# Order of the second modulation step and the planner's first transfer in a decoder block on one core

## The chip, the cores and the metric

The kernel runs on one core of a Trainium2 chip. The metric is the device time of one execution in microseconds (us), as the median of several runs; lower is better. A core has TensorE (PE, matmuls), VectorE (DVE), ScalarE (ACT), GpSimd (POOL) and SyncE (SP), which here issues every transfer from HBM. The engines run side by side, each through its own list of instructions, and wait for each other by semaphores.

## The reference, cut to what matters

One decoder block, 512 tokens of 1024 channels, float32. Around the change only this of it matters:

```
mod = silu(c) @ W_ada + b_ada                    # 6 x 1024 values
shift1, scale1, gate1, shift2, scale2, gate2 = split(mod, 6)
h = rms_norm(x, g_pre_mix) * (1 + scale1) + shift1
z = h @ w_in                                     # 1024 -> 4800 columns
...
```

Behind it come a GLU with a causal convolution of 31 taps and a LayerNorm, a latent attention of 8 heads, a gated merge, and an MLP of 4096 hidden channels; both sub-layers add to x. `h` can't be formed before `shift1` and `scale1` are there, and these need 2 of the 6 megabyte blocks of each 128 channels of `W_ada`.

## The kernel before, in words

**Layout.** Activations are held transposed, a tile being 128 channels by 512 tokens; `h` is 8 such tiles, k = 0 to 7. Float32 products are made of three fp32r products: every operand is split into a high part (an ACT copy that rounds) and a low part (a DVE subtraction), and `mm3` adds high x high, high x low and low x high.

**The first stage.** `x` is loaded (4 tiles), normed and transposed on PE into `xnT`. Then, for each k, three things follow each other:

- The modulation of step k: the shift and scale columns of its 128 channels, from one megabyte of `W_ada` (`ada_load`, 4 transfers of 256 KB). For k = 0 and 1 PE makes them, with 8 float32 matmuls of 256 columns against the column `cT` of silu(c); a matmul of this kind shows as two records in the trace. ACT copies the row out, and `to_columns` turns it into columns by two small matmuls with ones. For k = 2 to 7 DVE makes the sums with 8 operations over 128x256, and only the two ones matmuls are on PE.
- `h` of step k, in `first_products(k)`: ACT writes the high part from `xnT` with scale and shift; DVE (k = 0, 1) or ACT (k from 2) writes the exact value, and DVE subtracts for the low part.
- The first products with `h` of step k: a 128x896 piece of `w_in` (`g1_load`, two transfers of 256 and 192 KB) is split by ACT and DVE, and 21 matmuls of 512 columns add to 7 banks of PSUM over all k.

All `ro`, ones and column reads use one PSUM bank, `bg`, so modulation k+1 can write into it only after DVE has read the columns of k.

**What sets the order.** Nothing is emitted in program order. `Planner.record` notes every operation with a cost and its dependences; `Planner.plan` then plays the engines through in an event loop, and `Planner.issue` (line 410, the line of nearly every row) emits the instructions in the order so found. An engine that is free takes, of its operations that are ready, the one with the smallest key. For PE the key is the rank, which is the position in the program minus `plan.boost`; for all others it is the due time `dead` minus `plan.hurry`. Due times are followed back from the sums of PE costs in program order. Each transfer takes its turn on one modelled stream, `dma_free`, which says from when it is free. The arenas for buffers are laid out anew in up to 14 passes from the lives that the last plan gave, and the shortest plan is kept. The planner's costs set the order alone: on the chip each engine runs its list and waits where its operands are late.

**Lines.** `dma_free = 0.0` is line 341, in `Planner.plan`. In `emit`: `ada_load` 544, `g1_load` 558, `to_columns` 657, `first_products` 669; the loads of k = 0 and 1 lines 689 to 696, the loop with their modulation 698 to 708, the two calls of `first_products` 711 and 712, and the loop for k = 2 to 7 lines 714 to 736. Because of the boost of 1000 in line 689, all PE operations of both modulations rank ahead of the products of k = 0.

Of the kernel before, what the change touches and what calls it, by code (L numbers as in the profile page):

```python
# [53 lines left out]
HX, HA, HG, HC = 1.2e5, 1e5, 3e3, 1.1e5  # L54
# [115 lines left out]
class Planner:  # L170
# [17 lines left out]
    class Engine:  # L188
        def __init__(self, plan, name):
            self.plan, self.name = plan, name  # L190
# [134 lines left out]
    def plan(self):  # L325
        ops = self.ops
        pe_t = 0.0
        big = sum(o.cost for o in ops if o.eng == "pe") + TAIL
        for o in ops:
            o.dead = big  # L330
            if o.eng == "pe":
                pe_t += o.cost
                o.dead = pe_t
        for o in reversed(ops):
            lat = o.post + (2.0 * o.dma if o.dma else 0.0)
            for s in o.succ:
                q = ops[s]
                o.dead = min(o.dead, q.dead - q.cost - lat)
        heaps = {e: [] for e in self.NAMES}
        free = {e: 0.0 for e in self.NAMES}  # L340
        dma_free = 0.0
        landed = [0.0] * DEPTH
        future = []

        def key(o):
            return (o.rank, o.i) if o.eng == "pe" else (o.dead - o.hurry, o.i)

        for o in ops:
            o.ndep, o.ready = len(o.deps), 0.0
            if not o.ndep:  # L350
                heapq.heappush(future, (0.0, o.i))
        order = []
        now = 0.0
        while len(order) < len(ops):
            while future and future[0][0] <= now:
                o = ops[heapq.heappop(future)[1]]
                heapq.heappush(heaps[o.eng], (key(o), o.i))
            for e in self.NAMES:
                if free[e] <= now and heaps[e]:
                    o = ops[heapq.heappop(heaps[e])[1]]  # L360
                    o.t0 = now
                    free[e] = now + o.cost
                    if o.dma:
                        st = max(now + 1100.0, dma_free)
                        dma_free = st + o.dma
                        o.t1 = dma_free + 1100.0
                        landed.append(o.t1)
                        free[e] = max(free[e], landed[-DEPTH])
                    else:
                        o.t1 = free[e] + o.post  # L370
                    order.append(o)
                    for s in o.succ:
                        q = ops[s]
                        q.ndep -= 1
                        q.ready = max(q.ready, o.t1 if (q.eng != o.eng or o.dma) else free[e] if e == "pe" else max(free[e], o.t1 - 30))
                        if not q.ndep:
                            heapq.heappush(future, (q.ready, q.i))
            nxt = [free[e] for e in self.NAMES if free[e] > now and heaps[e]]
            if future:
                nxt.append(future[0][0])  # L380
            if not nxt:
                break
            now = max(now, min(nxt)) if min(nxt) > now else now
        assert len(order) == len(ops)
        self.length = max(o.t1 for o in ops)
        return order
# [28 lines left out]
def tile_hybrid_block(  # L415
# [48 lines left out]
    def emit(past, replay):  # L464
# [3 lines left out]
        plan = Planner(nc, dict(f_arena=fa, r_arena=ra, psum=pb))  # L468
        pe, act, dve, pool, sp = (plan.engine(e) for e in Planner.NAMES)

        def rf(b, pat=None, **kw):
            a = RTF[:, b[0]:b[0] + b[1]]
            return a.rearrange(pat, **kw) if pat else a
# [84 lines left out]
        def g1_load(k):  # L558
            b = fa.alloc((NA + NB) * P)
            sp.dma_start(out=fa.v(b)[:, :NA * P], in_=w_in[k * P:(k + 1) * P, 0:NA * P])  # L560
            sp.dma_start(out=fa.v(b)[:, NA * P:], in_=w_in[k * P:(k + 1) * P, D:D + NB * P])
            return b
# [84 lines left out]
        def hs(k, a=0, n=T):  # L647
            return ra.v(hT[k][0])[:, a:a + n], ra.v(hT[k][1])[:, a:a + n]
# [8 lines left out]
        def to_columns(src, lp, ks):  # L657

            for s in range(2):
                for i, k in enumerate(ks):  # L660
                    pe.matmul(pb.v(bg)[:, s * KD + k:s * KD + k + 1], lhsT=src[:, s, i * P:(i + 1) * P], rhs=ones[0:lp, 0:1],
                              start=True, stop=True)
            ksl = slice(ks[0], ks[-1] + 1)
            dve.tensor_tensor(mod[:, 0, ksl], pb.v(bg)[:, ksl], col("bada", ks[0], len(ks)), ALU.add)
            for k in ks:
                dve.scalar_tensor_tensor(mod[:, 1, k:k + 1], pb.v(bg)[:, KD + k:KD + k + 1], b1p[:, k:k + 1], col("gpm", k),
                                         op0=ALU.add, op1=ALU.mult)

        def first_products(k, wb):
            v = fa.alloc(T)  # L670
            act.activation(ra.v(hT[k][0]), xv[:, k], AF.Identity, scale=mod[:, 1, k:k + 1], bias=mod[:, 0, k:k + 1])
            if k < VDVE:
                dve.tensor_scalar(fa.v(v), xv[:, k], mod[:, 1, k:k + 1], mod[:, 0, k:k + 1], ALU.mult, ALU.add)
            else:
                act.activation(fa.v(v), xv[:, k], AF.Identity, scale=mod[:, 1, k:k + 1], bias=mod[:, 0, k:k + 1])
            dve.tensor_tensor(ra.v(hT[k][1]), fa.v(v), rf(hT[k][0]), ALU.subtract)
            fa.free(v)
            w = W(fa.v(wb, "p (s n) -> p s n", s=1), 1, (NA + NB) * P)
            fa.free(wb)

            for wi, hi in ((0, 0), (0, 1), (1, 0)):
                for i in range(NA + NB):
                    o = i // 2 if i % 2 == 0 else NA + i // 2
                    pe.matmul(pb.v(g1b[i]), lhsT=w(0, o * P, P)[wi], rhs=hs(k)[hi], start=k == 0 and wi + hi == 0,
                              stop=k == KD - 1 and wi == 1)
            w.free()
# [6 lines left out]
        wbs = []  # L693
# [2 lines left out]
            wbs.append(g1_load(k))  # L696
        plan.hurry = HG
        for k in range(2):
            av = ad0[k][1]
            ro = pb.v(bg)[0:1, 256:512].rearrange("p (s n) -> p s n", s=2)  # L700
            for j in range(KD):
                pe.matmul(ro, lhsT=cT[:, j:j + 1], rhs=av[:, :, j], start=j == 0, stop=j == KD - 1)
            fa.free(ad0[k][0])
            acc = fa.alloc(2 * P)
            accv = fa.v(acc, "p (s n) -> p s n", s=2)[0:1]
            act.copy(accv, ro)
            to_columns(accv, 1, (k,))
            fa.free(acc)
        plan.boost = 0
        plan.hurry = 0.0  # L710
        for k in range(2):
            first_products(k, wbs[k])

        for ks in KGRP:
            plan.hurry = HA - 1e4 * ks[0]
# [4 lines left out]
            wbs = [g1_load(k) for k in ks]  # L720
# [690 lines left out]
        for tp in range(2):  # L1411
# [34 lines left out]
            for k2 in range(KD // 2):  # L1446
                b = pb.alloc()
                for q in range(2):
                    for t in range(2):
                        k = 2 * k2 + q  # L1450
                        pe.transpose(pb.v(b)[:, (2 * q + t) * P:(2 * q + t + 1) * P], fa.v(xn[t])[:, k * P:(k + 1) * P], ident)
                for q in range(2):
                    k = 2 * k2 + q
# [280 lines left out]
        return plan  # L1734

    plan = emit({}, {})
    plan.plan()
    best = plan
    for _ in range(PASSES):
        try:  # L1740
            plan = emit(plan.lives(), {})
        except MemoryError:
            break
        plan.plan()
        if plan.length < best.length:
            best = plan
    if plan is not best:
        plan = emit({}, {n: a.places for n, a in best.spaces.items()})
# [31 lines left out]
```

## Time and profile before

| | |
|---|---|
| median of 3 runs | 816.17 us (815.13 to 816.69) |
| the profiled execution, its own time | 815.82 us |
| its span, first to last instruction | 814.0 us |
| granted TensorE clock, mean | 0.998 of 2.4 GHz |
| busy: PE, PE weight loads | 796.5 us (98%), 681.1 us (84%) |
| busy: DVE, ACT, POOL | 732.2 us (90%), 441.6 us (54%), 22.0 us (3%) |
| moved by the transfers | 117.31 MB |

The span is what the trace shows of the execution; 1.8 us of its own time lie around it. Matmuls are pipelined and their ends are modelled: a PE that shows busy is not always at its full rate, so the pitch (time between starts, from counts and starts) says more than the busy share. "x30" behind a row is the number of instructions merged in it, the first column its start and the second its length; what stands in brackets is the idle time of the engine before it, and what ended that.

### The profile page before, as it was taken

How to read it: one execution, taken by the hardware profiler on the slowest of the kernel's cores; microseconds unless marked ns; L12 is line 12 of the kernel's file. 1: busy time of each engine (PE TensorE's matmuls, PEld its weight loads, DVE VectorE, ACT ScalarE, POOL GpSimd, SP SyncE). 2: the span in 40 equal slices, each digit the busy share in tenths (PEclk: the TensorE clock that was granted, in tenths of full speed). 3: DMA queues.
4: the chain of work that ended last, by engine and by line, in shares of the span. 5: the costliest groups of instructions: out<-in, count | busy, mean ns of one | idle time of the engine just before them, and what ended most of it. 6: DMA issues, size and time to landing. Idle time of an engine off the chain costs nothing.

```text
span 814.0 us, 11293 instructions
## 1 busy us (share of the span) xinstructions
PE 796.5 (98%) x4222; PEld 681.1 (84%) x4222; DVE 732.2 (90%) x1049; ACT 441.6 (54%) x735; POOL 22.0 (3%) x77
## 2 busy tenths in 40 slices
PE   6999999999999999999999999999999999999996
PEld 3778988889897888878888889988998889888885
DVE  3898999999999999998899589899889989996696
ACT  5455453365885247237434387676665547554543
POOL 2001010000000000000000010000000000000001
PEclk9999999999999999999999999999999999999999
DMA  9989433112253250451799253026403580590302
GB/s 296 314 257 320 148 122 104 52 53 65 91 182 80 77 151 31 155 170 63 268 316 369 77 202 112 2 78 199 137 2 98 186 292 18 163 301 2 104 1 103
DMA packets 91337, 117.31 MB, mean 144 GB/s; under 512 B 7473, under 2 KB 66194, under 8 KB 91282
## 3 DMA queue, kind: packets, MB, share of 16 engines
q1 hardware_dynamic: 91282, 116.59, 44.9%
q8 instruction: 33, 0.54, 0.3%
q14 instruction: 22, 0.18, 0.1%
HBM read 108.18 MB, written 8.39 MB: 143 GB/s over the span
## 4 chain that ended last, share of the span: by engine, by line
PE 84%; DVE 8%; ACT 3%; DMA 2%; issue 1%; POOL 1%; SPq 0%; DVEq 0%
PE psum L410 84%; DVE f_arena L410 5%; DVE r_arena L410 3%; ACT f_arena L410 2%; ACT r_arena L410 1%; DMA c<-in_c_dram 1%; DMA f_arena<-in_w_in_dram 1%; POOL stats L410 1%; ACT stats L410 0%; SPq L410 0%; DMA rows<-in_kv_norm_g_dram 0%; DVE mod L410 0%; DVEq L1775 0%; DVEq L410 0%
## 5 line engine op out<-in xcount | busy, mean ns | idle before, releaser
L410 PE MATMUL psum<-r_arena 128*128 128x512 f32 (+3 forms) x3880 | 756.4, 355 | 0.9 <-ACT r_arena L410 0.6
L410 PEld LDWEIGHTS psum<-r_arena 128*128 128x128 f32 x3880 | 640.1, 189 | 100.7 <-ACT r_arena L410 2.6
L410 ACT CAST r_arena<-f_arena 128x1024 fp32r<-128x1024 f32 (+4 forms) x240 | 224.9, 964 | 169.1 <-PE psum L410 115.3
L410 DVE TENSOR_TENSOR r_arena<-f_arena,r_arena 128x1024 fp32r<-128x1024 f32 (+4 forms) x250 | 265.9, 1089 | 31.2 <-PE psum L410 21.4
L410 DVE SCALAR_TENSOR_TENSOR f_arena<-f_arena,cw 128x512 f32<-128x512 f32 x240 | 165.8, 738 | 0.0
L410 DVE TENSOR_TENSOR f_arena<-f_arena 128x1024 f32<-128x1024 f32 (+3 forms) x99 | 102.3, 1047 | 3.0 <-ACT r_arena L410 1.6
L410 ACT ACTIVATE f_arena<-f_arena 128x512 f32<-128x512 f32 (+4 forms) x112 | 66.1, 606 | 29.0 <-DVE f_arena L410 27.9
L410 ACT ACTIVATE f_arena<-psum 128x512 f32<-128x512 f32 x52 | 30.6, 594 | 71.9 <-PE psum L410 71.3
L410 DVE SCALAR_TENSOR_TENSOR f_arena<-f_arena,cT 128x256 f32<-128x256 f32 (+1 forms) x70 | 56.0, 801 | 7.4 <-DMA f_arena<-in_w_ada_dram 6.4
L410 DVE TENSOR_TENSOR f_arena<-psum,f_arena 128x512 f32<-128x512 f32 x64 | 42.9, 681 | 6.8 <-PE psum L410 6.8
L410 ACT COPY f_arena<-psum 128x512 f32<-128x512 f32 (+5 forms) x54 | 26.8, 517 | 33.2 <-PE psum L410 33.1
L410 PE MATMUL psum<-ident,f_arena 128*128 128x128 f32 x234 | 35.4, 291 | 8.2 <-DVE f_arena L410 8.1
L410 PEld LDWEIGHTS psum<-ident,f_arena 128*128 128x128 f32 x234 | 29.0, 149 | 14.1 <-DVE f_arena L410 9.3
L410 ACT CAST r_arena<-psum 128x512 fp32r<-128x512 f32 (+2 forms) x57 | 30.2, 563 | 12.1 <-PE psum L410 11.8
L410 DVE TENSOR_TENSOR r_arena<-psum,r_arena 128x512 fp32r<-128x512 f32 (+2 forms) x57 | 35.8, 654 | 0.6 <-ACT r_arena L410 0.3
L410 POOL TENSOR_TENSOR stats<-stats,nhalf 128x1 f32<-128x1 f32 (+1 forms) x17 | 13.3, 785 | 471.2 <-ACT stats L410 471.1
L410 ACT ACTIVATE r_arena<-f_arena 128x512 fp32r<-128x512 f32 (+3 forms) x20 | 13.0, 651 | 18.0 <-DVE f_arena L410 15.4
L410 ACT ACTIVATE r_arena<-f_arena,mod 128x512 fp32r<-128x512 f32 x8 | 6.5, 816 | 21.1 <-DVE mod L410 21.1
L410 DVE TENSOR_SCALAR f_arena<-f_arena,stats 128x1024 f32<-128x1024 f32 x8 | 6.0, 753 | 12.7 <-POOL stats L410 12.7
L410 DVE CUSTOM_DVE_ANT_0 f_arena<-psum,mask 128x128 f32<-128x128 f32 (+3 forms) x32 | 14.8, 481 | 0.1
L410 DVE SCALAR_TENSOR_TENSOR f_arena<-f_arena 128x512 f32<-128x512 f32 (+1 forms) x18 | 13.2, 740 | 0.0
L410 DVE SCALAR_TENSOR_TENSOR f_arena<-f_arena,psum 128x512 f32<-128x512 f32 x16 | 10.8, 678 | 2.2 <-ACT f_arena L410 2.2
(94 smaller groups left out, 182.9 us busy)
## 6 DMA issues: line engine op xcount, KB each, us to landing
f_arena<-in_w_ada_dram SPq DMA_DIRECT2D x16, 1024.0 KB
f_arena<-in_w_mlp_in_dram SPq DMA_DIRECT2D x32, 512.0 KB
f_arena<-in_w_mlp_out_dram SPq DMA_DIRECT2D x32, 512.0 KB
f_arena<-in_w_in_dram SPq DMA_DIRECT2D x24, 512.0 KB
f_arena<-in_w_ada_dram SPq DMA_DIRECT2D x32, 256.0 KB
f_arena<-in_x_dram SPq DMA_DIRECT2D x8, 512.0 KB
h_spill<-r_arena SPq DMA_DIRECT2D x16, 256.0 KB
f_arena<-in_w_attn_out_dram SPq DMA_DIRECT2D x8, 512.0 KB
```

Of the source, the lines that this page charges most:

```text
L410: getattr(self.real[o.eng], o.fn)(*o.a, **o.k)
```

## The change

It does two things. In the planner, the modelled stream of transfers is free from 1500 ns on instead of from 0. In the first stage the products of k = 0 are called between the modulations of k = 0 and of k = 1, and the boost holds for k = 0 alone, so that on PE the modulation of k = 1 ranks behind the products of k = 0 and ahead of those of k = 1. No operation is added or removed.

```diff
@@ Planner.plan
         free = {e: 0.0 for e in self.NAMES}
-        dma_free = 0.0
+        dma_free = 1500.0
         landed = [0.0] * DEPTH
@@ emit
         plan.hurry = HG
         for k in range(2):
+            plan.boost = 1000 * (1 - k)
             av = ad0[k][1]
             ro = pb.v(bg)[0:1, 256:512].rearrange("p (s n) -> p s n", s=2)
             for j in range(KD):
...
             act.copy(accv, ro)
             to_columns(accv, 1, (k,))
             fa.free(acc)
+            plan.boost = 0
+            plan.hurry = 0.0
+            first_products(k, wbs[k])
+            plan.hurry = HG
         plan.boost = 0
         plan.hurry = 0.0
-        for k in range(2):
-            first_products(k, wbs[k])
 
         for ks in KGRP:
```

## Rows read from the trace of the kernel before

**Rows 1.** Chain that ended last: start us, us, what.
```profile
19.81 23.67 PE psum L410 x110
...
61.20 121.92 PE psum L410 x667
...
197.86 6.19 DVE f_arena L410 x14
...
497.33 301.09 PE psum L410 x1680
```
**Rows 2.** Windows: busy us (x count) by engine, clock, DMA share, GB/s.
```profile
0.00:10.00 10.00, 2.26 (x10) 1.84 (x11) 1.70 (x4) 6.59 (x12) 4.46 (x47) 1.00 0.83 279
10.00:20.00 10.00, 9.81 (x47) 6.12 (x46) 4.19 (x11) 3.25 (x10) 1.51 (x3) 1.00 1.16 312
20.00:30.00 10.00, 10.00 (x46) 6.47 (x45) 8.34 (x16) 4.35 (x6) 0.12 (x1) 1.00 1.16 313
...
50.00:60.00 10.00, 10.00 (x48) 7.86 (x47) 9.79 (x21) 6.31 (x10) 0.18 (x2) 1.00 0.68 205
...
260.00:280.00 20.00, 20.00 (x90) 16.57 (x89) 20.00 (x28) 5.78 (x7) 0.00 (x0) 1.00 0.36 100
```
**Rows 3.** Timeline of PE from 9 to 66 us.
```profile
19.81 3.61 PE L410 MATMUL psum<-f_arena,cT 128*1 128x256 f32 x16 [0.19 <-DVE mod L410]
23.36 0.96 PE L410 MATMUL psum<-r_arena 128*128 128x512 f32 x3
24.25 0.60 PE L410 MATMUL psum<-ones,f_arena 1*128 1x1 f32 x4
24.78 7.14 PE L410 MATMUL psum<-r_arena 128*128 128x512 f32 x30
31.76 0.50 PE L410 MATMUL psum<-ones,f_arena 128*128 128x1 f32 x4
32.12 5.52 PE L410 MATMUL psum<-r_arena 128*128 128x512 f32 x23
...
59.47 6.78 PE L410 MATMUL psum<-r_arena 128*128 128x512 f32 x27
```
**Rows 4.** Timeline of ACT and DVE, 19 to 31 us, and step 7.
```profile
19.55 0.21 DVE L410 SCALAR_TENSOR_TENSOR mod<-psum,b1p,cols 128x1 f32<-128x1 f32 x1
...
19.85 0.81 ACT L410 ACTIVATE r_arena<-f_arena,mod 128x512 fp32r<-128x512 f32 x1 [0.46 <-DVE mod L410]
...
20.57 1.76 ACT L410 CAST r_arena<-f_arena 128x896 fp32r<-128x896 f32 x2
20.91 2.71 DVE L410 TENSOR_TENSOR r_arena<-f_arena,r_arena 128x512 fp32r<-128x512 f32 x3
...
23.52 0.36 ACT L410 COPY f_arena<-psum 1x256 f32<-1x256 f32 x1 [1.18 <-PE psum L410]
...
24.96 0.16 DVE L410 TENSOR_TENSOR mod<-psum,cols 128x1 f32<-128x1 f32 x1 [1.34 <-PE psum L410]
...
25.28 0.82 ACT L410 ACTIVATE r_arena<-f_arena,mod 128x512 fp32r<-128x512 f32 x1 [1.40 <-DVE mod L410]
...
25.74 0.35 DVE L410 TENSOR_SCALAR f_arena<-f_arena,cT 128x256 f32<-128x256 f32 x1
...
60.32 0.82 ACT L410 ACTIVATE r_arena<-f_arena,mod 128x512 fp32r<-128x512 f32 x1 [0.99 <-DVE mod L410]
```
**Rows 5.** Timeline of SP: the issues of the first transfers of w_ada and w_in.
```profile
3.80 7.20 SPq L410 DMA_DIRECT2D f_arena<-in_w_ada_dram  x7
...
11.05 1.31 SPq L410 DMA_DIRECT2D f_arena<-in_w_in_dram  x2
...
12.40 0.43 SPq L410 DMA_DIRECT2D f_arena<-in_w_ada_dram  x1
```
**Rows 6.** Windows at the end, one us each, columns as in rows 2.
```profile
806.00:807.00 1.00, 0.57 (x3) 0.14 (x1) 0.87 (x2) 0.73 (x3) 0.16 (x1) 1.00 0.64 242
...
810.00:811.00 1.00, 0.00 (x0) 0.00 (x0) 1.00 (x2) 0.00 (x0) 0.00 (x0) 0.50 0.73 270
```

## The prediction

> **What bounds the kernel now.** I read the chain of waits first. Nearly all of it is PE: from 61.20 us on it runs in long unbroken pieces on PE, with a stretch around 200 us that goes through DVE, and 301 us in one piece from 497 us [rows 1]. PE works at a steady rate there: the window from 260 us has 90 products in 20 us, a pitch of 0.222 us [rows 2]. Busy PE (796.5 us), the 7.6 us ahead of its first instruction and the 7.4 us behind its last leave some 2.5 us of the 814.0 us span in which PE sits idle in between. So the work on PE is fixed, and a change of order can only add or take waits.
>
> The change lies in the first 61 us, so the timelines of PE, ACT and DVE there come next. PE makes the modulation of step 0, then at 19.81 us, released by DVE's read of the columns, that of step 1 (16 records, 8 matmuls), then at 23.36 us the first products with h [rows 3]. Modulation 1 doesn't hold PE idle: it fills the time in which ACT and DVE make h of step 0. The high part of h is done at 19.85 + 0.81 = 20.66 us [rows 4]. The products could start there if their weights were split; the split was put behind h on ACT (20.57 us), so they could start at about 21.5 us, and PE takes them at 23.36. The two sides of the trade are seen here: products of step 0 up to 2.7 us earlier, and modulation 1, which all later steps follow, later.
>
> The products run at (31.76 - 24.78) / 30 = 0.2327 us each. The 18 of step 0 that are left at 24.78 us end at 24.78 + 18 x 0.2327 = 28.97 us, and those of step 1 follow at once, since their h has long been ready (25.28 + 0.82 = 26.10 us). PE is covered. From 30 us DVE is nearly full as well (9.79 of 10 us in the window from 50 us, rows 2), and h of step 7 comes from it: ACT ends it at 61.14 us, and the chain's long PE piece starts at 61.20 us [rows 1, 4].
>
> **What changes, part by part.** *The transfers.* Now SP issues the block of modulation 0, three quarters of that of modulation 1, then the first products' weights, then the last quarter [rows 5]. With the products of step 0 ahead in the program, modulation 1 is due 21 planned products later, and the weights of step 0 are due earlier by the planned modulation 1. So I expect the weights ahead of the whole block. Bytes up to and with the weights: 2.13 MB (x and small vectors) + 1.05 + 0.46 = 3.64 MB. At 279 and then 312 GB/s [rows 2] they are there at 10 + (3.64 - 2.79) / 312 GB/s = 12.7 us, and modulation 1's three quarters (4.42 MB) at 15.2 us. Both are wanted at 19.8 us or later. This costs nothing: the cover is the transposes and modulation 0, which hold PE until 19.4 us; without it each 0.26 MB late would be 0.8 us. It lets ACT and DVE split the weights of step 0 before h, in time that both now spend idle.
>
> *The start of the products of step 0.* The planner's costs set the order (they give no time). It gives a free PE the ready operation of lowest rank. When the columns of step 0 are read, modulation 1 is ready and the products aren't, as h takes one planned ACT operation with its latency (855 ns) against 434 ns for a modulation matmul. So one or two modulation matmuls go in front, I take two of eight; then the 21 products, then the other six. On the chip: two matmuls are 4 records, 19.81 + 4 x (23.36 - 19.81) / 16 = 20.7 us, just when the high part is ready. The products of step 0 run from 20.7 to 20.7 + 21 x 0.2327 = 25.6 us, the six from there to 25.6 + 12 x 0.222 = 28.25 us.
>
> *The new wait.* Behind the last modulation matmul comes a chain that the products of step 0 cover today and that nothing covers then. From where PE goes on (23.36 us) to the end of ACT's copy (23.52 + 0.36) and 0.05 us of release: 0.57 us. From the ones matmuls (24.25 us) over DVE's columns to the end of h (26.10 us) and 0.05 us: 1.90 us [rows 3, 4]. Together 2.47 us, so the products of step 1 start at 28.25 + 2.47 = 30.7 us against 28.97 now: 1.75 us later. PE has nothing else ready: all later products need h of later steps, and those stand behind the same bank's columns.
>
> *What comes back.* DVE now waits 1.34 us for the columns of step 1 and takes the sums of step 2 up at 25.74 us [rows 4]. Their data are there sooner: 6.19 MB are through at 20 + (6.19 - 5.91) / 313 GB/s = 20.9 us [rows 2]. Without the columns of step 1 ahead of them DVE can start when the low parts of step 0 and 1 are done, at 22.7 us (20.91 us, one of 0.69 and one of 1.08 us): a lead of 3.0 us. The ones of step 2 (32.12 - 31.76 = 0.36 us on PE, rows 3) then fall into the gap, and DVE no longer holds up steps 3 to 7. So from 30.7 us PE has 126 products of steps 1 to 6 and five times 0.36 us: 30.7 + 29.3 + 1.8 = 61.8 us for the start of step 7, now 61.20 us. (By the same count the kernel before would be there at 28.97 + 29.3 + 2.2 = 60.4 us; the 0.8 us are its waits for DVE.) **Sum: 0.6 us later.** Ends: at the steady pitch of 0.222 us the products take 28.0 us and step 7 starts 0.7 us earlier than now; if the 0.8 us of waits stay, it is 1.4 us later.
>
> *The planner's 1500 ns.* The modelled stream could not start before 1100 ns as it is, so all that hangs on transfers moves by 400 ns in the plan, and the order of the first stage stays. Due times don't move with it, so buffers may be placed otherwise, and later waits may come or go. No row prices this. Below, it can't gain more than the 2.5 us for which PE idles; above, I take as much again. I take nothing, being nearest to what a shift of all planned times does.
>
> The profiled execution has 815.82 us, the median 816.17 us. With 0.6 us the profiled sum is 816.4 us, and against the median 816.8 us. A measurement of this kernel can tell about 0.2%, 1.6 us, from no change.
>
> **The rivals.** *A, the forecast*, 0.42: 816.8 us, its own range 815.5 to 817.6.
>
> *B, the order on PE stays*, 0.06: if h of step 0 is planned so late that all eight matmuls still go in front, only the split of weights is earlier, and the time is 816.2 us. Against it: the high part of h takes 0.81 us, eight matmuls take 3.55 us.
>
> *C, faster: DVE's lead counts.* 0.20. The chain goes through DVE around 200 us [rows 1], and DVE is full from 40 us on. If DVE, not PE, paces the stretch from 25 to 245 us, its start 3.0 us earlier is worth that, less the 0.6 us: 816.17 - 3.0 + 0.6 = 813.8 us. It decides if DVE finds weights to split while it waits for the last first products. Against it: the convolution can start only behind these, and they end later.
>
> *D, slower: the columns of step 1 get stuck on DVE.* 0.29. They stand in DVE's list among the sums of steps 2 to 4. If a sum of step 4 is ahead of them, DVE waits for its block, 9.2 MB, at 20 + (9.2 - 5.91) / 313 GB/s = 30.5 us, where they are wanted at 29.4 us; and a low part of weights (1.08 us) may be in front as well. That is up to 2.2 us more in the gap, 819.0 us. It decides as soon as PE's gap exceeds 4 us. A worse placing of buffers would land about there too.
>
> *E, the clock.* 0.03. PE stands still for some 2 us in the gap. At the end of the kernel its last matmul ends at 806.57 us, and the granted clock is at half, 1.2 GHz, in the window from 810 us [rows 6]: idle for 3.4 us before it fell. If it fell here, 21 products at twice 0.2327 us would cost 4.9 us, 821.7 us. The Trainium skill (TensorE: Matmul & The Clock Gate, Part 1: The HAM clock gate) says that an idle engine is throttled to half clock and that only sustained activity releases it; by that rule the gap would be paid twice if it is long enough.
>
> **How the numbers follow.** B and nearly all of A are within 0.2%: 0.48. C is faster: 0.20. D and E are slower: 0.32. The likeliest is A, 816.8 us. The range reaches down to C's 813.8 and up to the forecast with the 2.5 us of a worse plan, 819.3 us; what lies outside is E, the far half of C and the end of D.
>
> **What would show it.** In the changed kernel's trace: SP issues two w_in transfers behind four of w_ada; PE has 4 records of modulation, then 21 products from 20.7 us, then 12 records; a hole of 2 to 2.5 us with the ones of steps 1 and 2 in it; products of step 1 from 30.7 us; sums of step 2 on DVE from 22.7 us; and a start of the last 21 first products within a microsecond of 61.8 us. I am wrong in the order if the 16 modulation records still stand together, wrong in the price if the hole is gone or above 4 us, and wrong about what follows if the shift at 61 us isn't the shift at the end.

## The result, and the profile after

The changed kernel takes 817.54 us in the median of 18 runs, the kernel before 815.19 us in 18 runs beside them: a ratio of 1.0028 with a 95% interval of 1.0022 to 1.0034, 2.3 us slower. The forecast was 0.6 us slower. The profiled execution of the changed kernel has a span of 815.7 us.

The timeline of PE in the changed kernel, in the stretch of [rows 3]:

```profile
19.26 1.02 PE L410 MATMUL psum<-f_arena,cT 128*1 128x256 f32 x4 [0.19 <-DVE mod L410]
20.22 5.05 PE L410 MATMUL psum<-r_arena 128*128 128x512 f32 x21
25.20 2.75 PE L410 MATMUL psum<-f_arena,cT 128*1 128x256 f32 x12
28.46 0.60 PE L410 MATMUL psum<-ones,f_arena 1*128 1x1 f32 x4 [0.51 <-ACT f_arena L410]
29.89 0.60 PE L410 MATMUL psum<-ones,f_arena 128*128 128x1 f32 x4 [0.84 <-DVE f_arena L410]
30.36 8.22 PE L410 MATMUL psum<-r_arena 128*128 128x512 f32 x28
38.42 0.50 PE L410 MATMUL psum<-ones,f_arena 128*128 128x1 f32 x4
```

The order is the forecast one to the record: 4 records of modulation 1, the 21 products of step 0, the other 12 records, a hole with the ones of steps 1 and 2 in it, the products of step 1. These start at 30.36 us; 30.7 us was forecast. What wasn't forecast stands in the next row. 28 products take 38.42 - 30.36 = 8.06 us, 0.288 us each, against the 0.2327 us of [rows 3]. No engine made PE wait there, as the windows over this stretch show (busy us and count of PE, PE weight loads, DVE, ACT and POOL, then clock, DMA share, GB/s):

```profile
28.00:30.00 2.00, 0.71 (x5) 0.62 (x5) 0.84 (x4) 0.88 (x2) 0.00 (x0) 1.00 1.20 293
30.00:30.50 0.50, 0.50 (x5) 0.50 (x5) 0.50 (x2) 0.30 (x1) 0.00 (x0) 0.87 1.23 307
30.50:33.50 3.00, 3.00 (x7) 2.33 (x8) 2.93 (x9) 2.35 (x3) 0.12 (x1) 0.50 1.07 319
33.50:34.00 0.50, 0.50 (x3) 0.46 (x2) 0.50 (x2) 0.00 (x0) 0.00 (x0) 0.72 1.20 301
34.00:36.00 2.00, 2.00 (x11) 1.64 (x10) 1.95 (x4) 0.00 (x0) 0.12 (x1) 1.00 1.16 309
```

The granted clock, the third number from the end, is full (2.4 GHz) in the hole, falls to half (1.2 GHz) just as the products begin, and is full again from 34 us on. What each window lost gives the time at half clock: 0.13 + 3.00 + 0.28 = 3.4 us, from about 30.37 to 33.78 us, so 1.7 us of PE work. That is most of the 2.3 us. PE shows as fully busy all the while; only the clock column and the count of products tell.

The rest of the first stage, on SP and DVE:

```profile
3.89 4.20 SPq L410 DMA_DIRECT2D f_arena<-in_w_ada_dram  x4
9.39 0.82 SPq L410 DMA_DIRECT2D f_arena<-in_w_in_dram  x2
10.26 2.27 SPq L410 DMA_DIRECT2D f_arena<-in_w_ada_dram  x4
```
```profile
21.99 0.35 DVE L410 TENSOR_SCALAR f_arena<-f_arena,cT 128x256 f32<-128x256 f32 x1
22.38 3.09 DVE L410 SCALAR_TENSOR_TENSOR f_arena<-f_arena,cT 128x256 f32<-128x256 f32 x6
25.38 1.08 DVE L410 TENSOR_TENSOR r_arena<-f_arena,r_arena 128x896 fp32r<-128x896 f32 x1
29.16 0.16 DVE L410 TENSOR_TENSOR mod<-psum,cols 128x1 f32<-128x1 f32 x1 [2.70 <-PE psum L410]
```

The weights of step 0 come ahead of modulation 1's block, unlike in [rows 5], and DVE starts the sums of step 2 at 21.99 us instead of 25.74 us [rows 4]. Then it stands for 2.70 us in front of the columns of step 1, with one of the eight sums still behind them.

The chain that ended last, start and length in us, runs through PE from 29.89 us on, with no long stretch on DVE around 200 us as in [rows 1]:

```profile
29.89 151.58 PE psum L410 x800
...
181.51 64.42 PE psum L410 x410
...
246.59 115.35 PE psum L410 x524
...
498.36 301.25 PE psum L410 x1680
```

### The profile page after: what moved, and what is told of

Read it like the earlier page. It is cut to its first block, busy times and chain, and to the rows that moved or that the text cites. A ratio compares the mean times of both kernels' runs of the same rounds, so it can differ in the third digit from the quotient of the medians.

```text
span 815.7 us, 11287 instructions
## 1 busy us (share of the span) xinstructions
PE 796.6 (98%) x4222; PEld 682.4 (84%) x4222; DVE 732.4 (90%) x1049; ACT 441.9 (54%) x735; POOL 25.0 (3%) x77
## 4 chain that ended last, share of the span: by engine, by line
PE 93%; ACT 3%; DVE 2%; DMA 1%; POOL 1%; issue 0%; SPq 0%; DVEq 0%; ACTq 0%
PE psum L410 93%; DVE f_arena L410 2%; ACT f_arena L410 2%; ACT r_arena L410 1%; DMA c<-in_c_dram 1%; POOL stats L410 1%; ACT stats L410 0%; SPq L410 0%; DVEq L1778 0%; DVE mod L410 0%; DVEq L410 0%; DVE r_arena L410 0%; ACTq L410 0%
## 5 line engine op out<-in xcount | busy, mean ns | idle before, releaser
L410 ACT CAST r_arena<-f_arena 128x1024 fp32r<-128x1024 f32 (+5 forms) x240 | 225.2, 964 | 169.2 <-PE psum L410 112.4
L410 ACT ACTIVATE f_arena<-f_arena 128x512 f32<-128x512 f32 (+3 forms) x112 | 66.1, 607 | 30.0 <-DVE f_arena L410 29.1
L410 POOL TENSOR_TENSOR stats<-stats,nhalf 128x1 f32<-128x1 f32 (+1 forms) x17 | 15.4, 907 | 481.3 <-ACT stats L410 481.2
```

The source lines that it names most:

```text
L410: getattr(self.real[o.eng], o.fn)(*o.a, **o.k)
```

## The experiments

All were timed in turn with the kernel before. Since an execution's first transfers don't always land alike (last section), stages of profiles are compared from the start of modulation 1 on PE. "First GLU" is ACT's first tanh behind the first products, "last DVE" the end of DVE's last operation. Two pairs of traces of one program each (before and start only; the changed kernel and its repetition, with 47.76 us) agree within 0.03 us at the first GLU; at the later points before and start only differ by 0.7 us.

| kernel | ratio to before, 95% interval | modulation 1, us | to first GLU | to 497 us piece of the chain | to last DVE |
|---|---|---|---|---|---|
| before | | 19.81 | 45.34 | 477.52 | 791.20 |
| changed | 1.0028 (1.0022 to 1.0034) | 19.26 | 47.73 | 479.10 | 792.94 |
| start only | 0.9998 (0.9990 to 1.0007) | 18.25 | 45.36 | 478.20 | 791.88 |
| hole filled | 1.0004 (0.9995 to 1.0012) | 19.15 | 46.20 | 477.62 | 791.49 |
| front half filled | 1.0023 (1.0013 to 1.0033) | 19.50 | 47.88 | 479.17 | 792.98 |
| back half filled | 1.0005 (0.9997 to 1.0014) | 19.66 | 46.13 | 477.55 | 791.38 |
| modulation 1 in front | 0.9994 (0.9986 to 1.0003) | 19.91 | 45.23 | 477.28 | 790.96 |
| cover | 1.0014 (1.0005 to 1.0022) | 20.43 | 45.65 | 477.86 | 791.74 |
| cover, sums first | 1.0012 (1.0003 to 1.0020) | 19.43 | 44.94 | 478.01 | 791.77 |

**Half of the change: the planner's first transfer alone.**

```diff
@@ Planner.plan, kernel before
-        dma_free = 0.0
+        dma_free = 1500.0
```

> The order of before, only the modelled stream of transfers free from 1500 ns on. Theory 1 (the loss is PE's hole between the products of step 0 and 1, and the granted clock that falls behind it): no effect, a ratio to before of 1.000 within 0.001, granted clock as before. Theory 2 (the planner's 1500 ns moves buffers or later operations, and this is the loss): 816.5 us or more, a ratio of 1.002 or above.

Measured: 0.9998. The instruction lists of all five engines come out the same as before's, with the same waits; and the order change with `dma_free = 0.0` gives the changed kernel's lists. So this half of the change does nothing, Theory 2 falls, and this run's trace is a second one of the kernel before.

**The hole filled.** Six matmuls with zeros, adding nothing to a PSUM bank that is being summed anyway, are emitted into the hole, past the planner. All other lists stay as in the changed kernel.

```diff
@@ changed kernel, Planner.__init__
-        self.slack = 0.0
+        self.slack, self.fill = 0.0, {}
@@ Planner.issue
             getattr(self.real[o.eng], o.fn)(*o.a, **o.k)
+            for _ in range(self.fill.get(o.i, 0)):
+                self.zero()
@@ emit, behind the modulation matmuls
+            if k:
+                plan.fill[len(plan.ops) - 1] = 2
+                plan.zero = lambda: nc.tensor.matmul(pb.v(g1b[0])[:, 0:P], lhsT=mask[:, 0:P], rhs=ident, start=False, stop=False)
@@ emit, behind to_columns
+            if k:
+                plan.fill[len(plan.ops) - 3] = 4
```

> The changed kernel with 6 small matmuls with zeros (128x128, float32, 0.22 us each) emitted into PE's hole, 2 ahead of the ones matmuls of step 1 and 4 behind them; nothing else of the order differs. Theory 1 (half clock behind the hole, 3.4 us long in the changed kernel's trace, costs 1.7 us): the granted clock is full from 20 to 60 us, the products of step 1 still start at about 30.4 us, and the time falls by 1.3 to 1.9 us against the changed kernel, to about 815.9 us (ratio to before 1.0005 to 1.0015). Rival (the later start of step 1 and the other order behind it are the loss, the clock is a detail): 817.3 us or more, a ratio above 1.002.

Measured: 1.0004, 815.96 us. The timeline of PE in this kernel, in which a zero matmul shows as two records, and two windows behind the hole:

```profile
27.77 0.71 PE L708 MATMUL psum<-ident,mask 128*128 128x128 f32 x4
28.41 0.60 PE L410 MATMUL psum<-ones,f_arena 1*128 1x1 f32 x4
28.94 1.16 PE L708 MATMUL psum<-ident,mask 128*128 128x128 f32 x8
29.93 0.52 PE L410 MATMUL psum<-ones,f_arena 128*128 128x1 f32 x4
30.32 6.63 PE L410 MATMUL psum<-r_arena 128*128 128x512 f32 x28
36.78 0.50 PE L410 MATMUL psum<-ones,f_arena 128*128 128x1 f32 x4
...
57.98 8.46 PE L410 MATMUL psum<-r_arena 128*128 128x512 f32 x36
```
```profile
30.00:32.00 2.00, 2.00 (x12) 1.73 (x12) 1.96 (x7) 1.44 (x3) 0.12 (x1) 1.00 0.99 296
32.00:34.00 2.00, 2.00 (x10) 1.67 (x9) 1.96 (x5) 1.17 (x2) 0.00 (x0) 1.00 1.02 305
```

The products of step 1 start no earlier, at 30.32 us, and the zeros are work that nobody needs. But the 28 products take 36.78 - 30.32 = 6.46 us, 1.60 us less than in the changed kernel, and the granted clock is 1.00 in every window of the stage. From modulation 1 to the last DVE operation it is 792.94 - 791.49 = 1.45 us shorter. By the ratios to before the filling is worth about 2.0 us, give or take 0.8 us. Theory 1 holds; the rival falls.

**The changed kernel once more, and half of the hole filled.** The same emission, with the 2 zeros ahead of the ones of step 1 alone, or the 4 behind them alone.

```diff
@@ front half: hole filled
-                plan.fill[len(plan.ops) - 3] = 4
+                pass
@@ back half: hole filled
-                plan.fill[len(plan.ops) - 1] = 2
```

> The changed kernel once more, on the same chip as the three beside it. Theory 1: as measured, about 2.3 us above before (ratio 1.0022 to 1.0034), mean granted clock 0.996 in most runs, that is some 3.3 us at half clock more than before. Rival (its loss belonged to the chip or the runs of the first measurement): a ratio below 1.0015.

Measured: 1.0026 (1.0017 to 1.0034), 817.74 us. Of the 30 runs of the changed kernel so far, 27 have a mean granted clock of 0.996 or less; the kernel before has 0.997 to 0.999. (This mean also holds the half clock behind the last matmul, some 3.7 us of the profiled execution's span.) Of the three with 0.998, two took 815.04 and 814.62 us, the fastest of the 30; the third, 817.32 us, is not explained by this. The four with 0.994 took 818.30 us or more. The trace of the repetition has the same hole, and 3.4 us at half clock behind it.

> Only the first half second of PE's hole filled: 2 of the 6 zero matmuls, behind the last modulation matmul; the 0.84 us between the ones of step 1 and of step 2 stay idle. Theory 1a (the idle time summed over the hole brings the clock down): with 0.84 of 1.35 us idle left the clock may fall still, in part of the runs; ratio to before between 1.0010 and 1.0030. Theory 1b (any half of the hole is short enough alone): full clock, ratio 1.0000 to 1.0010.

Measured: 1.0023, with a clock of 0.996 in all 8 runs. Timeline of PE and windows:

```profile
28.17 0.71 PE L708 MATMUL psum<-ident,mask 128*128 128x128 f32 x4
28.81 0.60 PE L410 MATMUL psum<-ones,f_arena 1*128 1x1 f32 x4
30.25 0.61 PE L410 MATMUL psum<-ones,f_arena 128*128 128x1 f32 x4 [0.84 <-DVE f_arena L410]
30.72 8.25 PE L410 MATMUL psum<-r_arena 128*128 128x512 f32 x28
```
```profile
30.00:32.00 2.00, 1.75 (x8) 1.52 (x9) 2.00 (x7) 1.44 (x3) 0.12 (x1) 0.77 1.08 325
32.00:34.00 2.00, 2.00 (x7) 1.52 (x6) 1.93 (x5) 1.56 (x3) 0.00 (x0) 0.50 1.18 309
34.00:36.00 2.00, 2.00 (x9) 1.64 (x8) 1.97 (x4) 0.00 (x0) 0.13 (x1) 0.87 1.15 313
```

> Only the back part of the hole filled: 4 zero matmuls between the ones of step 1 and of step 2; the 0.5 us behind the last modulation matmul stay idle. Theory 1a (summed idle time): less idle left than with the front filled, so full clock in more runs; ratio 1.0000 to 1.0015. Theory 1b: full clock in all, ratio 1.0000 to 1.0010. If the clock falls here and not with the front filled, the idle time next to the one-column modulation matmuls is what counts.

Measured: 1.0005, clock 0.997 or 0.998 in 10 of 11 runs. Timeline of PE:

```profile
28.85 0.60 PE L410 MATMUL psum<-ones,f_arena 1*128 1x1 f32 x4 [0.51 <-ACT f_arena L410]
29.39 1.16 PE L707 MATMUL psum<-ident,mask 128*128 128x128 f32 x8
30.38 0.52 PE L410 MATMUL psum<-ones,f_arena 128*128 128x1 f32 x4
30.76 6.62 PE L410 MATMUL psum<-r_arena 128*128 128x512 f32 x28
```

The 28 products take 37.22 - 30.76 = 6.46 us, as with the whole hole filled. The two fillings come apart, and 1b falls: with 0.84 us left idle the clock falls, with 0.51 us it doesn't. 1a fits both, but idle time is not all in which they differ. With the front filled, PE has neither products nor zeros for 30.72 - 28.88 = 1.84 us; with the back filled for 29.39 - 28.34 = 1.05 us; in the changed kernel for 30.36 - 27.95 = 2.41 us. Whether the idle time, the length of this stretch or its place in the hole decides, these runs don't tell: the ones matmuls stand in both halves and the one-column modulation matmuls ahead of them, and no run left either out. Nor does the fall come in the pause itself: by the windows it comes at 30.37 us in the changed kernel, with the first product at 30.36 us, and at 31.08 us with the front filled, 0.36 us behind the first product.

**Modulation 1 in front.** The changed program, but PE makes all of modulation 1 ahead of the products of step 0, as before. Behind the first stage the order is before's on every engine.

```diff
@@ changed kernel, emit
-            plan.boost = 1000 * (1 - k)
+            plan.boost = 1000
```

> The changed program, but with the boost of 1000 for both modulations, so that PE makes all of modulation 1 ahead of the products of step 0 as before; the weights of step 0 still come ahead of modulation 1's block. Theory 1: no hole, full clock, 814.6 to 815.3 us (ratio 0.9990 to 1.0003), below before if the early split of the weights takes DVE's waits away. Rival (the transfers' new order is the loss): 816.5 us or more.

Measured: 0.9994, and in a second set of runs:

> The front run once more, to see whether it beats the kernel before: its profile shows 0.1 to 0.25 us less from modulation 1's start on than before's. Theory 1 (no hole, so nothing is lost, and the early split of the weights gives DVE a little): ratio 0.999 to 1.000. Rival (the weights' earlier place costs later blocks as much): ratio 1.000 to 1.001.

Measured: 0.9996 (0.9987 to 1.0005). The transfers' new order stays in this kernel, SP issuing the weights of step 0 ahead of modulation 1's block, and costs nothing: the rivals fall. The chain's long pieces start where before's do:

```profile
61.18 121.93 PE psum L410 x667
...
497.19 301.09 PE psum L410 x1680
```

It is the best version found, and by both intervals not to be told from before.

**The hole covered by products.** Two modulation matmuls in front, seven products, the other six, then fourteen products over the chain to step 1.

```diff
@@ changed kernel, emit
         for k in range(2):
-            plan.boost = 1000 * (1 - k)
+            mark = len(plan.ops) - 14.5
+            plan.boost = 1000
...
             for j in range(KD):
+                if k:
+                    plan.boost = len(plan.ops) - mark
```

> The changed program, with modulation 1 ranked behind 7 of the 21 products of step 0: two of its matmuls in front, six behind 7 products, 14 products left to cover the chain to step 1. Theory 1: no hole and full clock; the products of step 0 start at 20.2 us and those of step 1 by 28.8 us; 814.3 to 815.2 us (ratio 0.999 to 1.000). Rival (any later modulation 1 delays all steps behind it, or the newly laid out order later in the kernel is the loss): 816.5 us or more, ratio above 1.0015.

Measured: 1.0014, slower than Theory 1 had it and just short of the rival's 1.0015. In the profiled execution PE has no hole and the clock is full through the stage, but to the first GLU it takes 45.65 us, 0.3 us more than before. (That execution took 817.49 us, 1.1 us above the median; in 5 of the 11 runs the mean clock is 0.996, so that a fall of the clock in some of them is not excluded.) DVE's timeline shows a likely reason why the earlier products bring nothing:

```profile
23.54 0.48 DVE L410 SCALAR_TENSOR_TENSOR f_arena<-f_arena,cT 128x256 f32<-128x256 f32 x1
27.48 0.16 DVE L410 TENSOR_TENSOR mod<-psum,cols 128x1 f32<-128x1 f32 x1 [3.46 <-PE psum L410]
```

DVE's list has two of the sums of step 2 ahead of the columns of step 1, and DVE, which is busy for 9.75 of the 10 us from 50 us on, waits for these with six sums undone. The planner had the transfers land later, by its clock, than the chip has them; on the chip they are there.

**Cover, and the sums first.** The planner is told that these blocks land 2.5 us earlier.

```diff
@@ cover run, Planner.plan
-                        o.t1 = dma_free + 1100.0
+                        o.t1 = dma_free + 1100.0 - (2500.0 if 2e4 < o.hurry < 9.9e4 else 0.0)
```

> Modulation 1 behind 7 products as in the cover run, and the planner told that the blocks of W_ada and w_in of the first stage land 2.5 us earlier than it has them (on the chip PE is some 3 us behind the plan there, the transfers aren't), so that DVE makes 7 of the 8 sums of step 2 ahead of the columns of step 1. Theory (DVE in its fixed list lost its lead of 3.5 us in the cover run waiting for these columns): that wait falls below 1 us, the first stage ends 0.3 to 0.8 us earlier after modulation 1's start than before's 45.3 us, and the time is 814.7 to 815.4 us, a ratio of 0.9990 to 1.0000. Rival (PE's pitch in the first stage or later stages set the time, DVE's lead is worth nothing): ratio 1.0005 or more.

Measured: 1.0012. Half of the theory held: the longest wait for columns falls from 3.5 to 0.9 us, as the waits of the cover run and of this one show (total, times, longest, in us),

```profile
DVE mod L410 <- PE psum L410: 3.7, 2, 3.5
```
```profile
DVE mod L410 <- PE psum L410: 1.4, 3, 0.9
```

and the first stage is 0.4 us shorter than before's, and 0.7 us shorter than in the cover run, 44.94 us. But by the start of the chain's last long piece it is 0.5 us behind, and the time is 0.8 us above before, which is the rival's range. Both cover runs, like the changed kernel, have another order in later stages than before. Whether that order costs what the first stage gives stays open: no run kept the later order fixed, and two executions of before's lists (before, start only) differ by 0.7 us there themselves.

## Why the prediction was right or wrong

**The order and the wait: right.** The two matmuls in front, the weights' earlier place, the hole and its length (2.4 us) came as worked out. Products of step 1 start 30.36 - 19.26 = 11.10 us after modulation 1, 1.94 us later than before's 28.97 - 19.81 = 9.16 us; 1.75 us were forecast. With the hole filled, 0.86 us of this are left at the first GLU (46.20 against 45.34), so about 1.1 us come back by then, as the step "what comes back" had it (1.75 - 0.6 = 1.15 us). At full clock, then, the sum holds within 0.3 us at the place for which it was worked out. At the end the filled kernel is only 0.3 us behind (1.0004), for a reason that the sum doesn't have: from the first GLU to the last long piece of the chain the four kernels with the changed order take 431.29 to 431.42 us, the three with before's later order 432.05 to 432.84 us.

The start of the last 21 first products was to lie within a microsecond of 61.8 us. In the changed kernel they are the last of this row:

```profile
59.62 8.46 PE L410 MATMUL psum<-r_arena 128*128 128x512 f32 x36
```

Behind its first 15 products, 3.5 us, they start at about 63.1 us; that sign failed. With the hole filled, they start at about 57.98 + 3.5 = 61.5 us.

One reading of the prediction is off, without weight in the sum: the steady pitch of 0.222 us counts all 90 products that touch the window from 260 us. Their row in the trace of before is a little longer than that window:

```profile
259.72 20.56 PE L410 MATMUL psum<-r_arena 128*128 128x512 f32 x90
```

That is about 0.227 us each, with which the early end for step 7 would have been 0.1 us ahead of now instead of 0.7 us.

**DVE's lead: half right.** It starts the sums of step 2 at 21.99 us (22.7 us forecast), but gives 2.7 us back waiting for the columns of step 1. The 3.0 us of lead in the sum existed only for the sums of step 2. As PE doesn't wait for DVE from step 1 to step 7 in the filled kernel, this cost nothing that its trace shows.

**Case A was taken with full clock, and that step failed.** The sum has no term for the clock. Rival E, with a chance of 0.03, is what happened, on top of A: 3.4 us at half clock behind the hole. The Trainium skill (TensorE: Matmul & The Clock Gate, Part 1: The HAM clock gate) says that an engine with too little to do falls to half clock and that work brings it back; the trace agrees, with half clock from 30.37 us and full clock again at 33.78 us under products. The mistake was in weighing the end of the kernel [rows 6], where 3.4 us pass between the last matmul and the fall, as if that were the least that it takes. Here PE idles for 0.51 and 0.84 us, with 8 records of ones matmuls between and behind, and the clock falls in nearly every run. Even at the end of the kernel the 3.4 us belong to that one execution. In the trace of cover, sums first, the last matmuls and two windows behind them are these:

```profile
799.80 6.96 PE L410 MATMUL psum<-r_arena 128*128 128x512 f32 x30
```
```profile
807.00:808.00 1.00, 0.00 (x0) 0.00 (x0) 1.00 (x3) 0.02 (x1) 0.72 (x1) 1.00 0.62 238
808.00:809.00 1.00, 0.00 (x0) 0.00 (x0) 1.00 (x2) 0.97 (x3) 0.00 (x0) 0.86 0.07 25
```

The clock falls at 808.72 us, 2.0 us behind the last matmul's end at 806.76 us; with the front half filled it falls 4.7 us behind. The hole's 2.4 us lie well within that spread. E's price was too high, 4.9 us for all 21 products: half clock held for 3.4 us and cost 1.6 us.

**The rivals C and D.** DVE's lead didn't make the kernel faster (C), and the columns did not get stuck behind a sum of step 4 (D): the hole stayed at 2.4 us. The 2.3 us fall into D's stretch of the range by another cause, so that the time lies in the range is luck. The absolute forecast, 816.8 us, also looks nearer than it was: it was counted from a median of 3 runs, 816.17 us, where 18 runs gave 815.19 us.

**The planner's 1500 ns: right at nothing**, shown by the lists and a run. The 2.5 us above the forecast, kept for it, were partly used by the clock instead.

## What to carry to other kernels

Count a pause on TensorE twice where the products behind it are dense: once as time, once as a possible 1.6 us at half clock, and read the clock column in windows of half a microsecond, since busy time doesn't show it. A hand-over chain through ACT and DVE belongs under other matmuls; where there are none, a few matmuls with zeros in its last part kept the clock full here (1.0005 instead of 1.0023 to 1.0028). And before moving work on the engine that shows busy, look at the other engines' fixed lists too: products that start earlier were worth nothing in the cover run, and the stage was 0.7 us shorter once DVE's list had the sums ahead of the columns.

## What the runs showed of the hardware that was not expected

A stretch of 1.84 us without products, in which PE idles for 0.84 us at most and has ones matmuls around that, was followed by 3.4 us at half clock; one of 1.05 us with 0.51 us idle was not. Behind the last matmul of the kernel the fall came after 2.0 to 4.7 us in the eleven traces. Where the first transfers land moves the start by more than half of what the change costs: the same lists began modulation 0 at 14.20 us in one execution and at 12.86 us in another (start only), and modulation 1 at 19.81 and 18.25 us.
